# One decoder step on one core: the second value projection is moved from ahead of the attention to among its first scores

## The chip, the cores and the metric

The kernel runs on one core of one Trainium2 chip. The metric is device time in microseconds (us) of one launch. Besides the times there is one profiled execution of the kernel before, and all instants below ("at 628.7") are microseconds from the start of the span of that execution.

## The reference, cut to what matters

A prompt of 512 positions and 8 single-token samples (520 columns together, `T`) go through two layers of width 1024. The part that matters here is the start of the second layer: keys and values are made once from a normed hidden state, queries from another one, and 16 query heads share 4 key/value heads within a window of 128.

```python
hk = rmsnorm(h, kv_norm_g)
k = rope_partial((hk @ w_k).reshape(B, T, N_KV_HEADS, HEAD_DIM), pos)
v = (hk @ w_v).reshape(B, T, N_KV_HEADS, HEAD_DIM)
hn = rmsnorm(h, norm_mix_g[i])
q = rope_partial((hn @ w_q[j]).reshape(B, T, N_HEADS, HEAD_DIM), pos)
o = swa_prompt(q, k, v, sinks[j])        # window 128, softmax with a sink per head
h = h + o @ w_o[j]
```

Before it stand a gated short convolution, a feed-forward block and a gated per-layer embedding; after it another feed-forward block, another gate and a last norm. All of it is in the changed kernel as it was.

## The kernel before, in words

**Products.** Every matrix product is made of three single-pass products of split operands (high with high, high with low, low with high). `dense` (L192) loads one 128-column tile of weights by a DMA from the SP queue into one of three `raw` buffers, and splits it in halves of four 128x128 blocks: ACT casts the high part (L180), DVE subtracts for the low part (L162). The split halves lie in a ring of four `pair` buffers, so that a tile's first half can be split when the tile two before it has been used up that far. TensorE (PE) then runs 8 k-steps of 6 matmuls (128x260): 48 matmuls a tile. `ps2` hands out the accumulation banks A, B, C in rotation; once `banks["tags"]` is "AB" (L969) it hands out A and B alone, and C holds attention scores (`s`).

**The stretch around the change.** In order: two key tiles (`k0`, `k1`, L735); two value tiles (`v0`, `v1`, L750) from the same input `kx`; four transpositions of the first value tile (`vsplit`, L758, tile `vps`); query tiles `q0` to `q3` (L963) from input `mx`; then the attention of the first half of the heads. A finished value tile is multiplied by the norm's factor `r` on DVE into `vt` (L753), and its last columns are written out by a DMA. Keys and queries are turned by `rope` (L711): a shuffle and a product on DVE, a product and a sum on POOL (for `q2` and `q3` on DVE instead), then a split of the result by two casts on ACT and two subtractions on DVE (`ksplit` L723 into `kk` and `kk1`, `qsplit` L780). The tiles `q2` and `q3` are first copied from their bank by ACT (`to_sbuf`, L204, tiles `q2s`, `q3s`).

**The attention** goes in units u = 0 to 15 (8 for each half of the heads): scores on PE (L805), mask and row maximum on DVE (L810), exponentials on ACT (L822), normalising on ACT (L831) and POOL (L833), transpositions on PE (`pt`, L843), their split on ACT and DVE (`PT`, L844 and L845), and the products with the values (`av`, L856). Query tiles `q4` to `q7` are filler there: `steps` (L928) is a generator that yields after each k-step, and `pump(n)` runs n steps of it. `AHEAD` says how many steps come before the first score, `FILL` how many at each of four places of each unit. At u = 6 what is left of them is run, and the second value tile is transposed. The second half of the heads (u = 8 on) needs `kk1` and the queries `q4` to `q7`. The output projections (`o`, L960) fill units 8 on.

**What sets the order.** The program is written in this order; a scheduler then sets the order in which the instructions stand on each engine, and each engine runs its own in that order.

Of the kernel before, what the change touches and what calls it, by code (L numbers as in the profile page):

```python
# [23 lines left out]
KD = D // 128  # L24
# [23 lines left out]

AHEAD = 7
FILL = ((1, 3, 1, 9), (1, 0, 0, 0), (0, 2, 2, 1), (0, 1, 0, 1),  # L50
# [9 lines left out]
def _program(nc, a, o):  # L60
# [3 lines left out]
    with tile.TileContext(nc) as tc, ExitStack() as ctx:  # L64
# [297 lines left out]
        for j in range(KD):  # L362
            pc = pc1 if j == 1 else dense(a["w_in"][3 * j], cx, f"pc{j}") if j else None
            px_ = dense(a["w_in"][3 * j + 1], cx, f"px{j}") if j else None
            if j == 0:
                r = nm.r
# [311 lines left out]
        px, pe, nq = ffn(0, fx, nf)  # L678
        kx, mx = dpairs(KD, 0, "kx"), dpairs(KD, 7, "mx")
        nk = Norm("k")  # L680
# [68 lines left out]
        preload(AF.Exp, kt32[0])  # L749
        for p in range(2):  # L750
            pv = dense(a["w_v"][p], kx, f"v{p}")
            t = cp.tile([128, T], F32, tag="r2", name="vt1") if p else temp("vt0")
            V.tensor_tensor(halves(t), pv, halves(r), ALU.mult)  # L753
            nc.sync.dma_start(o["vw"][:, p, :], t[:, S - WIN:])
            G.tensor_copy(vsm[:, p, :], t[:, S:])
            vt.append(t)

        def vsplit(p, tag):  # L758
# [169 lines left out]
        def steps(tiles):  # L928

            def load(i):
                w, _, name = tiles[i][:3]
                raw = wr.tile([128, 8, 128], F32, tag="raw", name=f"{name}r")
                nc.sync.dma_start(raw[:, :w.shape[1]], w)
                return raw[:, :w.shape[1]]

            def cast(raw, k, name):
                pr = wp.tile([128, 2, 4, 128], F32R, tag="pair", name=f"{name}p{k}")
                A.copy(pr[:, 0], raw[:, k:k + 4])  # L940
                V.tensor_tensor(pr[:, 1], raw[:, k:k + 4], pr[:, 0].bitcast(F32), ALU.subtract)
                return [(pr[:, 0, i, :], pr[:, 1, i, :]) for i in range(4)]

            n = len(tiles)
            raws = [load(0), load(1)]
            ws = [p for k in range(0, raws[0].shape[1], 4) for p in cast(raws[0], k, tiles[0][2])]
            yield
            for i, (_, xs, name, done) in enumerate(tiles):
                ps, cur, ws = ps2(name), ws, []
                if i + 2 < n:  # L950
                    raws.append(load(i + 2))
                for k in range(len(cur)):
                    dense_k(ps, cur, xs, k)
                    if i + 1 < n and k in (1, 3) and 4 * (k // 2) < raws[i + 1].shape[1]:
                        ws += cast(raws[i + 1], 4 * (k // 2), tiles[i + 1][2])
                    if k == len(cur) - 1:
                        done(ps[:, :, :TH])
                    yield
# [4 lines left out]
        for t_ in range(4):  # L963
            if t_ == 2:
                kk1 = ksplit(1, [[cp.tile([128, T], F32R, tag=g, name=f"kk1{g}") for g in gs]
                                 for gs in (("tabc", "tabs"), ("acc", "r"))], kt32[1])
            pq_ = dense(a["w_q"][t_], mx, f"q{t_}")
            qsplit(t_, qrope(t_, to_sbuf(pq_, f"q{t_}s") if t_ > 1 else pq_))
        banks["tags"] = "AB"  # L969
        o0 = otiles(0, "D3", "D10")  # L970

        pending = []
# [7 lines left out]
        def add_h(m):  # L980
            return lambda ps: later(1, V.tensor_tensor, halves(h[m]), halves(h[m]), ps, ALU.add)

        gen = steps([(a["w_q"][t_], mx, f"q{t_}", q_done(t_)) for t_ in range(4, 8)]
                    + [wo_tile(0, m, *o0, add_h(m)) for m in range(KD)])
        next(gen)
        left = 4 * KD

# [7 lines left out]
        def pump(n):  # L995
# [4 lines left out]
            left -= min(n, left)  # L1000

        att = [Attn(0, kk0, vv0, *o0), None]
        samples = [sample(0, "X6", "X7", *o0), None]
# [13 lines left out]

        pump(AHEAD)
        each("score", 0)
# [195 lines left out]
```

## Time and profile before

| | us |
|---|---|
| median of 3 runs (lowest to highest) | 1227.99 (1227.5 to 1228.44) |
| the profiled execution's own time | 1226.76 |
| its span, first to last instruction | 1225.0 |
| PE busy / idle in the span | 1201.0 / 24.0 |
| DVE, ACT, POOL busy | 876.2, 630.9, 112.9 |
| mean granted clock of TensorE | 0.994 |

A granted clock of 1.00 is TensorE's 2.4 GHz, 0.50 its 1.2 GHz. The page's shares are means over the whole kernel; the change touches some 120 us of it, from the key projections at 605 to the last score that needs a query tile at 712.

### The profile page before, as it was taken

The numbers are of one execution on the slowest core, as the hardware profiler recorded it, in microseconds if no ns is written. First come the engines' busy times: TensorE is split into PE (matmuls) and PEld (weight loads), VectorE is DVE, ScalarE is ACT, GpSimd is POOL, SyncE is SP. The second block draws the span as 40 slices with busy tenths as digits, with TensorE's granted clock in tenths as the row PEclk, the third lists the DMA queues.
The fourth block names the chain that finished last, engine by engine and source line by source line (L and its number), as shares of the span: only waits on it lengthen the run. The fifth ranks groups of instructions, "written<-read, shape, count | busy, mean of one in ns | idle before, by whom it ended". The sixth has DMA issues, their size and how long they took to land.

```text
span 1225.0 us, 23933 instructions
## 1 busy us (share of the span) xinstructions
PE 1201.0 (98%) x9805; PEld 1183.9 (97%) x9805; DVE 876.2 (72%) x1509; ACT 630.9 (52%) x1073; POOL 112.9 (9%) x155
## 2 busy tenths in 40 slices
PE   9999999999999999999998989999999999999996
PEld 8999999999999999999998979999999999999996
DVE  6845557877777873678788777787776779428955
ACT  6323244555555842465655787654555567226631
POOL 2000000101010000111033321000101010001000
PEclk9999999999999999999999999999999999999998
DMA  6223323856655342744631131346666643248302
GB/s 217 87 87 96 97 87 106 214 147 155 157 156 139 92 127 91 204 99 116 185 114 53 39 92 53 113 119 184 154 159 154 161 99 115 93 132 210 116 1 70
DMA packets 56862, 149.69 MB, mean 122 GB/s; under 512 B 5680, under 2 KB 18992, under 8 KB 56752
## 3 DMA queue, kind: packets, MB, share of 16 engines
q1 hardware_dynamic: 46144, 117.66, 30.6%
q0 software_dynamic: 10464, 30.46, 13.6%
q8 instruction: 77, 1.26, 0.4%
q14 instruction: 33, 0.27, 0.1%
q10 hardware_dynamic: 144, 0.03, 0.0%
HBM read 113.10 MB, written 4.58 MB: 96 GB/s over the span
## 4 chain that ended last, share of the span: by engine, by line
PE 87%; DVE 7%; ACT 2%; DMA 1%; issue 1%; POOL 1%; SPq 0%; DVEq 0%; ACTq 0%; POOLq 0%
PE d L189 13%; PE pb L503 12%; PE pd L503 8%; PE pa L503 8%; PE o L189 4%; PE pg L189 4%; PE po L189 4%; PE g L189 4%; PE u L189 4%; PE pg L214 3%; PE pc L189 3%; PE pb L189 3%; PE px L189 3%; PE pbd L503 3%; PE pdd L503 2%; PE pad L503 1%
## 5 line engine op out<-in xcount | busy, mean ns | idle before, releaser
L503 PE MATMUL pb<-xs,wh 128*128 128x260 f32 x864 | 158.9, 283 | 0.0
L503 PEld LDWEIGHTS pb<-xs,wh 128*128 128x128 f32 x864 | 133.4, 188 | 0.0
L162 DVE TENSOR_TENSOR wl<-s,wh 128x1024 fp32r<-128x1024 f32 x72 | 88.0, 1223 | 37.4 <-PE pb L503 27.7
L453 ACT CAST wh<-s 128x1024 fp32r<-128x1024 f32 x72 | 75.7, 1051 | 73.1 <-PE pd L503 53.8
L503 PE MATMUL pd<-xs,wh 128*128 128x260 f32 x576 | 106.9, 285 | 0.2 <-DVE u L512 0.2
L503 PE MATMUL pa<-xs,wh 128*128 128x260 f32 x576 | 105.3, 283 | 0.0
L503 PEld LDWEIGHTS pd<-xs,wh 128*128 128x128 f32 x576 | 88.7, 188 | 1.8 <-DVE u L512 0.4
L503 PEld LDWEIGHTS pa<-xs,wh 128*128 128x128 f32 x576 | 88.8, 188 | 0.0
L503 PE MATMUL pb<-xs,wl 128*128 128x260 f32 x288 | 81.5, 283 | 0.0
L503 PE MATMUL pd<-xs,wl 128*128 128x260 f32 x288 | 81.4, 283 | 0.0
L503 PEld LDWEIGHTS pd<-xs,wl 128*128 128x128 f32 x288 | 54.2, 188 | 0.0
L503 PEld LDWEIGHTS pb<-xs,wl 128*128 128x128 f32 x288 | 54.2, 188 | 0.0
L503 PE MATMUL pa<-xs,wlE 128*128 128x260 f32 x144 | 40.7, 283 | 0.0
L503 PE MATMUL pa<-xs,wl 128*128 128x260 f32 x144 | 40.7, 283 | 0.0
L503 PE MATMUL pb<-xs,wlE 128*128 128x260 f32 x144 | 40.6, 282 | 0.0
L512 DVE TENSOR_TENSOR u<-pd,u 128x520 f32<-128x520 f32 x36 | 25.0, 695 | 21.7 <-PE pd L503 21.7
L160 POOL DMA_DIRECT2D wlE<-w1r x18 | 15.4, 857 | 229.4 <-ACT wlE L159 229.4
L453 ACT CAST wh<-w3r 128x1024 fp32r<-128x1024 f32 x18 | 18.9, 1052 | 26.9 <-PE pb L503 26.9
L822 ACT ACTIVATE P<-P,nmx 128x256 f32<-128x256 f32 (+1 forms) x64 | 30.2, 475 | 2.3 <-DVE nmx L814 2.2
L453 ACT CAST wh<-w1r 128x1024 fp32r<-128x1024 f32 x18 | 18.9, 1052 | 22.2 <-PE pb L503 22.2
L214 PE MATMUL pg<-px1D,wg 128*128 128x260 f32 x216 | 28.5, 284 | 0.0
L503 PEld LDWEIGHTS pa<-xs,wlE 128*128 128x128 f32 x144 | 27.2, 189 | 0.0
(1066 smaller groups left out, 3372.4 us busy)
## 6 DMA issues: line engine op xcount, KB each, us to landing
w1r<-in_w_gu SPq DMA_DIRECT2D x18, 512.0 KB, 3.5
w0r<-in_w_gu SPq DMA_DIRECT2D x18, 512.0 KB, 3.6
w2r<-in_w_gu SPq DMA_DIRECT2D x18, 512.0 KB, 3.5
wlE<-w1r POOLq DMA_DIRECT2D x18, 512.0 KB, 5.6
w3r<-in_w_gu SPq DMA_DIRECT2D x18, 512.0 KB, 3.6
wlE<-w3r POOLq DMA_DIRECT2D x18, 512.0 KB, 4.5
h<-in_xT SPq DMA_DIRECT2D x8, 260.0 KB, 5.6
xs<-xn POOLq DMA_DIRECT2D x4, 520.0 KB, 6.6
```

What stands on the lines that cost most here:

```text
L160: G.dma_start(out=dst, in_=src, accum_op=ALU.add)
L162: V.tensor_tensor(dst, src, hi.bitcast(F32), ALU.subtract)
L189: TE.matmul(ps[:, c, :TH], l, r[:, c * TH:(c + 1) * TH], start=(k == 0 and i == 0), stop=(k == len(ws) - 1 and i == 2))
L214: TE.matmul(ps, l, r[:, cols], start=(k == 0 and i == 0), stop=(k == n - 1 and i == 2))
L453: A.copy(hi, src)
L503: TE.matmul(ps[:, e, :TH], w[l][:, e, k, :], x[r][:, k, :], start=(start and k == 0 and q == 0), stop=(k == 3 and q == 2), skip_group_chec ...
L512: V.tensor_tensor(dst, ps, src, ALU.add)
L822: A.activation(P[:, j, :w], P[:, j, :w], AF.Exp, bias=nmx[:, j:j + 1], accum_out=sm[:, j:j + 1])
```

## The change

- `v1` is no longer computed behind `v0`. It is the first tile of the generator `steps`, ahead of `q4`. What is done with a finished value tile is now a function, `vout`, called by hand for `v0` and by the generator for `v1`.
- `AHEAD` is 8, the 8 k-steps of `v1`; `FILL` has 5 steps where it had 3 in its first row. The generator has 40 steps before the output projections (`left = 5 * KD`) where it had 32.
- The input `kx` now lies in E2 to E5, D3 and D10, where it lay in E2 to E5, E0, E1 and D3. E0 and E1 are the buffers of the attention's `P`. The attention's output buffers (D3 and D10, `otiles`) are taken only behind the 8 steps.
- A part of `kk1` lies in a new buffer "r3" and not in that of `r`, which `v1` still reads.

```diff
--- before.py
+++ after.py
@@ -46,8 +46,8 @@
 
 
 
-AHEAD = 7
-FILL = ((1, 3, 1, 9), (1, 0, 0, 0), (0, 2, 2, 1), (0, 1, 0, 1),
+AHEAD = 8
+FILL = ((1, 5, 1, 9), (1, 0, 0, 0), (0, 2, 2, 1), (0, 1, 0, 1),
         (1, 2, 4, 1), (0, 2, 0, 6), (2, 0, 0, 1), (9, 0, 0, 6),
         (2, 5, 4, 0), (6, 0, 1, 3), (0, 0, 1, 3), (0, 1, 1, 2),
         (0, 1, 0, 1), (0, 2, 2, 3), (1, 0, 0, 2), (1, 0, 0, 1),
@@ -676,7 +676,8 @@
             po = dense(a["w_out"][m], yx, f"po{m}")
             resid(m, po, nf, (N_FFN0,), (fx,))
         px, pe, nq = ffn(0, fx, nf)
-        kx, mx = dpairs(KD, 0, "kx"), dpairs(KD, 7, "mx")
+        kx = dpairs(4, 0, "kx") + dpairs(2, 6, "kx") + dpairs(2, 13, "kx")
+        mx = dpairs(KD, 7, "mx")
         nk = Norm("k")
         pg = {}
         for i in range(KD + 1):
@@ -747,13 +748,15 @@
             prep(mx[k], N_MIX1, k)
         vt = []
         preload(AF.Exp, kt32[0])
-        for p in range(2):
-            pv = dense(a["w_v"][p], kx, f"v{p}")
+
+        def vout(p, pv):
             t = cp.tile([128, T], F32, tag="r2", name="vt1") if p else temp("vt0")
             V.tensor_tensor(halves(t), pv, halves(r), ALU.mult)
             nc.sync.dma_start(o["vw"][:, p, :], t[:, S - WIN:])
             G.tensor_copy(vsm[:, p, :], t[:, S:])
             vt.append(t)
+
+        vout(0, dense(a["w_v"][0], kx, "v0"))
 
         def vsplit(p, tag):
 
@@ -941,17 +944,16 @@
                 V.tensor_tensor(pr[:, 1], raw[:, k:k + 4], pr[:, 0].bitcast(F32), ALU.subtract)
                 return [(pr[:, 0, i, :], pr[:, 1, i, :]) for i in range(4)]
 
-            n = len(tiles)
             raws = [load(0), load(1)]
             ws = [p for k in range(0, raws[0].shape[1], 4) for p in cast(raws[0], k, tiles[0][2])]
             yield
             for i, (_, xs, name, done) in enumerate(tiles):
                 ps, cur, ws = ps2(name), ws, []
-                if i + 2 < n:
+                if i + 2 < len(tiles):
                     raws.append(load(i + 2))
                 for k in range(len(cur)):
                     dense_k(ps, cur, xs, k)
-                    if i + 1 < n and k in (1, 3) and 4 * (k // 2) < raws[i + 1].shape[1]:
+                    if i + 1 < len(tiles) and k in (1, 3) and 4 * (k // 2) < raws[i + 1].shape[1]:
                         ws += cast(raws[i + 1], 4 * (k // 2), tiles[i + 1][2])
                     if k == len(cur) - 1:
                         done(ps[:, :, :TH])
@@ -963,12 +965,10 @@
         for t_ in range(4):
             if t_ == 2:
                 kk1 = ksplit(1, [[cp.tile([128, T], F32R, tag=g, name=f"kk1{g}") for g in gs]
-                                 for gs in (("tabc", "tabs"), ("acc", "r"))], kt32[1])
+                                 for gs in (("tabc", "tabs"), ("acc", "r3"))], kt32[1])
             pq_ = dense(a["w_q"][t_], mx, f"q{t_}")
             qsplit(t_, qrope(t_, to_sbuf(pq_, f"q{t_}s") if t_ > 1 else pq_))
         banks["tags"] = "AB"
-        o0 = otiles(0, "D3", "D10")
-
         pending = []
 
         def later(n, fn, *args):
@@ -980,10 +980,11 @@
         def add_h(m):
             return lambda ps: later(1, V.tensor_tensor, halves(h[m]), halves(h[m]), ps, ALU.add)
 
-        gen = steps([(a["w_q"][t_], mx, f"q{t_}", q_done(t_)) for t_ in range(4, 8)]
-                    + [wo_tile(0, m, *o0, add_h(m)) for m in range(KD)])
+        tiles = [(a["w_v"][1], kx, "v1", lambda ps: vout(1, ps))]
+        tiles += [(a["w_q"][t_], mx, f"q{t_}", q_done(t_)) for t_ in range(4, 8)]
+        gen = steps(tiles)
         next(gen)
-        left = 4 * KD
+        left = 5 * KD
 
         def run_pending(every=False):
             for job in pending:
@@ -999,6 +1000,9 @@
                 next(gen, None)
             left -= min(n, left)
 
+        pump(AHEAD)
+        o0 = otiles(0, "D3", "D10")
+        tiles += [wo_tile(0, m, *o0, add_h(m)) for m in range(KD)]
         att = [Attn(0, kk0, vv0, *o0), None]
         samples = [sample(0, "X6", "X7", *o0), None]
         event = 0
@@ -1015,7 +1019,6 @@
             if 0 <= u < 16:
                 getattr(att[u // 8], what)(u % 8, *args)
 
-        pump(AHEAD)
         each("score", 0)
         tick(-1, 0)
         each("exps", 0)
```

The scheduler's orders before and after differ from here to u = 8. On DVE, behind the ropes of the two key tiles (`v0p`, `q0p`: halves of split weights; `kk`, `kk1`: split keys; `vt`: a value tile), this stood before:

```order
L162 TENSOR_TENSOR v1p_7279<-v1r_7274,v1p_7279 128x512
L730 TENSOR_TENSOR kk_7343<-k0b,kk_7343 64x520 x2
L753 TENSOR_TENSOR vt_7269<-v_7212,rk 128x520
L730 TENSOR_TENSOR kk_7343<-k0b,kk_7343 64x520 x2
L162 TENSOR_TENSOR q0p_7355<-q0r_7353,q0p_7355 128x512
L162 TENSOR_TENSOR q0p_7358<-q0r_7353,q0p_7358 128x512
L730 TENSOR_TENSOR kk1tabs<-k_7186,kk1tabc 64x520
L162 TENSOR_TENSOR q1p_7424<-q1r_7422,q1p_7424 128x512
L730 TENSOR_TENSOR kk1tabs<-k_7186,kk1tabc 64x520
L753 TENSOR_TENSOR vt_7330<-v_7273,rk 128x520
L162 TENSOR_TENSOR q1p_7427<-q1r_7422,q1p_7427 128x512
L767 TENSOR_TENSOR vv_7334<-vps_7336,vv_7334 128x4x2x64
```

and this stands there now:

```order
L162 TENSOR_TENSOR q0p_7296<-q0r_7291,q0p_7296 128x512
L731 TENSOR_TENSOR kk_7281<-k0b,kk_7281 64x520 x2
L754 TENSOR_TENSOR vt_7268<-v_7211,rk 128x520
L731 TENSOR_TENSOR kk_7281<-k0b,kk_7281 64x520 x2
L162 TENSOR_TENSOR q1p_7362<-q1r_7360,q1p_7362 128x512
L770 TENSOR_TENSOR vv_7272<-vps_7274,vv_7272 128x4x2x64
L162 TENSOR_TENSOR q1p_7365<-q1r_7360,q1p_7365 128x512
L731 TENSOR_TENSOR kk1tabs<-k_7185,kk1tabc 64x520 x2
L731 TENSOR_TENSOR kk1r_7431<-k_7185,kk1acc 64x520 x2
L162 TENSOR_TENSOR q2p_7443<-q2r_7441,q2p_7443 128x512
L714 STREAM_SHUFFLE q0a<-q_7290 128x520
```

The half of `v1`'s weights has been replaced by that of `q0`, both stand-alone halves of `q0` and the second `vt` are gone from here, and the first `vt` has kept its place behind two splits of `kk`.

On PE, at the start of `q0`, this stood before:

```order
L189 MATMUL v_7273<-kxE_6314,v1p_7279 128x260 x6
L189 MATMUL v_7273<-kxD_6315,v1p_7279 128x260 x12
L764 MATMUL vps_7336<-ident,vt_7269 128x128 x4
L189 MATMUL q_7352<-mxD_6316,q0p_7355 128x260 x12
L189 MATMUL q_7352<-mxD_6317,q0p_7355 128x260 x12
```

and now:

```order
L189 MATMUL v_7211<-kxE_6312,v0p_7214 128x260 x6
L189 MATMUL v_7211<-kxD_6313,v0p_7217 128x260 x12
L189 MATMUL v_7211<-kxD_6314,v0p_7217 128x260 x12
L189 MATMUL q_7290<-mxD_6315,q0p_7293 128x260 x8
L767 MATMUL vps_7274<-ident,vt_7268 128x128 x4
L189 MATMUL q_7290<-mxD_6315,q0p_7293 128x260 x4
L189 MATMUL q_7290<-mxD_6316,q0p_7293 128x260 x12
```

The transpositions of `vt` stood behind all 48 matmuls of `v1`; now they stand behind 8 matmuls of `q0`.

On PE, from the last query tile of the first half to the next ones (`s` are scores, from one `q` each), this stood before:

```order
L189 MATMUL q_7573<-mxD_6318,q3p_7579 128x260 x12
L189 MATMUL q_7573<-mxD_6319,q3p_7579 128x260 x12
L805 MATMUL s_7707<-kk_7343,q_7416 128x128 x2
L805 MATMUL s_7707<-kk_7343,q_7485 128x128 x2
L189 MATMUL q_7656<-mxD_6316,q4p_7650 128x260 x12
L189 MATMUL q_7656<-mxD_6317,q4p_7650 128x260 x12
L189 MATMUL q_7656<-mxD_6318,q4p_7653 128x260 x12
L189 MATMUL q_7656<-mxD_6319,q4p_7653 128x260 x6
L805 MATMUL s_7707<-kk_7343,q_7568 128x128 x2
L805 MATMUL s_7707<-kk_7343,q_7639 128x128 x2
L189 MATMUL q_7656<-mxD_6319,q4p_7653 128x260 x6
L189 MATMUL q_7765<-mxD_6316,q5p_7671 128x260 x5
```

and now:

```order
L189 MATMUL q_7511<-mxD_6318,q3p_7517 128x260 x12
L808 MATMUL s_7655<-kk_7281,q_7354 128x128 x2
L808 MATMUL s_7655<-kk_7281,q_7423 128x128 x2
L189 MATMUL v_7592<-kxE_6309,v1p_7586 128x260 x6
L189 MATMUL v_7592<-kxE_6310,v1p_7586 128x260 x6
L189 MATMUL v_7592<-kxE_6311,v1p_7586 128x260 x6
L189 MATMUL v_7592<-kxE_6312,v1p_7586 128x260 x6
L189 MATMUL v_7592<-kxD_6313,v1p_7589 128x260 x12
L189 MATMUL v_7592<-kxD_6314,v1p_7589 128x260 x12
L808 MATMUL s_7655<-kk_7281,q_7506 128x128 x2
L808 MATMUL s_7655<-kk_7281,q_7577 128x128 x2
L189 MATMUL q_7675<-mxD_6315,q4p_7607 128x260 x12
```

and on DVE, from the rope of `q3` to the first mask, before:

```order
L714 TENSOR_TENSOR q3a<-q3a,rope 128x520
L941 TENSOR_TENSOR q5p_7686<-q5r,q5p_7686 128x512
L717 TENSOR_TENSOR q3b<-q3b,q3a 128x520
L786 TENSOR_TENSOR q_7639<-q3b,q_7639 64x520 x2
L941 TENSOR_TENSOR q6p_7780<-q6r,q6p_7780 128x512
L810 ISA P_7716,mxs_7717<-s_7707,mask 128x128
```

and now:

```order
L944 TENSOR_TENSOR q4p_7622<-q4r,q4p_7622 128x512
L718 TENSOR_TENSOR q3b<-q3b,q3a 128x520
L789 TENSOR_TENSOR q_7577<-q3b,q_7577 64x520 x2
L944 TENSOR_TENSOR q5p_7715<-q5r,q5p_7715 128x512
L754 TENSOR_TENSOR vt_7649<-v_7592,rk 128x520
L944 TENSOR_TENSOR q5p_7730<-q5r,q5p_7730 128x512
L813 ISA P_7664,mxs_7665<-s_7655,mask 128x128
```

`v1` has taken the place of `q4` behind the first scores, and its `vt` stands ahead of the first mask.

On PE, around the end of `q7`, this stood before:

```order
L189 MATMUL q_8119<-mxD_6319,q7p_8041 128x260 x12
L843 MATMUL pt_8272<-ident,P_8150 128x128 x4
L856 MATMUL av_8279<-PT_8180,vv_7334 128x512
L856 MATMUL av_8279<-PT_8181,vv_7334 128x512
L856 MATMUL av_8279<-PT_8180,vv_7334 128x512 x2
L856 MATMUL av_8279<-PT_8181,vv_7334 128x512
L856 MATMUL av_8279<-PT_8180,vv_7334 128x512
L805 MATMUL s_8304<-kk_7343,q_7416 128x256 x2
L805 MATMUL s_8304<-kk_7343,q_7485 128x256 x2
L805 MATMUL s_8304<-kk_7343,q_7568 128x256 x2
L843 MATMUL pt_8297<-ident,P_8150 128x128 x4
L805 MATMUL s_8304<-kk_7343,q_7639 128x256 x2
```

and now:

```order
L189 MATMUL q_8210<-mxD_6317,q7p_8079 128x260 x12
L846 MATMUL pt_8254<-ident,P_8101 128x128 x4
L189 MATMUL q_8210<-mxD_6318,q7p_8079 128x260 x12
L859 MATMUL av_8278<-PT_8131,vv_7272 128x512
L859 MATMUL av_8278<-PT_8132,vv_7272 128x512
L859 MATMUL av_8278<-PT_8131,vv_7272 128x512 x2
L859 MATMUL av_8278<-PT_8132,vv_7272 128x512
L859 MATMUL av_8278<-PT_8131,vv_7272 128x512
L846 MATMUL pt_8296<-ident,P_8101 128x128 x4
L808 MATMUL s_8303<-kk_7281,q_7354 128x256 x2
L808 MATMUL s_8303<-kk_7281,q_7423 128x256 x2
L808 MATMUL s_8303<-kk_7281,q_7506 128x256 x2
```

One group of four transpositions (`pt`) stood behind the last of `q7` and stands ahead of its last 12 matmuls now.

## Rows read from the trace of the kernel before

**Rows 1.** Busy time by engine, from the page (share of the span, instructions).
```profile
PE 1201.0 (98%) x9805; PEld 1183.9 (97%) x9805; DVE 876.2 (72%) x1509; ACT 630.9 (52%) x1073; POOL 112.9 (9%) x155
```

**Rows 2.** Busy time in four stretches: stretch, its length, engines, PEclk, DMA share, GB/s.
```profile
604.00:655.89 51.89, 50.73 (x423) 50.18 (x421) 44.47 (x78) 27.24 (x47) 15.60 (x16) 1.00 0.45 132
655.89:670.15 14.26, 12.14 (x96) 11.49 (x97) 11.99 (x38) 7.85 (x24) 5.66 (x9) 1.00 0.14 50
670.15:703.11 32.96, 32.85 (x240) 30.63 (x239) 25.31 (x93) 24.98 (x74) 11.83 (x19) 0.95 0.08 26
703.11:720.89 17.78, 13.76 (x82) 10.64 (x82) 15.55 (x55) 14.75 (x45) 6.85 (x13) 1.00 0.52 147
```

**Rows 3.** The three longest waits of PE, 620 to 722: total us, times, longest.
```profile
PE pt L843 <- ACT P L831: 2.5, 2, 2.0
PE pt L843 <- DVE PT L845: 2.2, 4, 1.0
PE q L189 <- ACT q3s L204: 1.0, 1, 1.0
```

**Rows 4.** Timeline of PE, 625 to 643: start, length, what, [idle before, releaser].
```profile
625.10 4.50 PE L189 MATMUL v<-kxE,v1p 128*128 128x260 f32 x36
...
630.87 0.60 PE L764 MATMUL vps<-ident,vt 128*128 128x128 f32 x4
631.23 5.97 PE L189 MATMUL q<-mxD,q0p 128*128 128x260 f32 x48
637.04 5.92 PE L189 MATMUL q<-mxD,q1p 128*128 128x260 f32 x48
```

**Rows 5.** Timeline of DVE, 625 to 638.
```profile
625.40 2.27 DVE L730 TENSOR_TENSOR kk<-k0b,kk 64x520 fp32r<-64x520 f32 x2 [0.31 <-ACT kk L728]
627.71 0.70 DVE L753 TENSOR_TENSOR vt<-v,rk 128x520 f32<-128x520 f32 x1
...
630.17 1.29 DVE L162 TENSOR_TENSOR q0p<-q0r,q0p 128x512 fp32r<-128x512 f32 x2
...
637.39 0.75 DVE L713 STREAM_SHUFFLE q0a<-q 128x520 f32<-128x520 f32 x1
```

**Rows 6.** Instructions of L764: the semaphore that its weight loads pass (lengths, instants).
```profile
L764 PEldq EVENT_SEMAPHORE  x1: 51/51/51, 628.7 to 628.7; - x1
```

**Rows 7.** Timeline of PE, 654 to 660.
```profile
654.35 0.56 PE L805 MATMUL s<-kk,q 128*128 128x128 f32 x4
655.89 4.33 PE L189 MATMUL q<-mxD,q4p 128*128 128x260 f32 x34 [0.98 <-ACT q3s L204]
```

**Rows 8.** Timeline of ACT, 653 to 656.
```profile
653.94 1.28 ACT L784 CAST q<-q2b 64x520 fp32r<-64x520 f32 x2 [1.62 <-DVE q2b L717]
655.24 0.59 ACT L204 COPY q3s<-q 128x520 f32<-128x520 f32 x1
```

**Rows 9.** First unit: the split of q3 and the first mask (DVE), the first transposition (PE).
```profile
659.90 1.42 DVE L786 TENSOR_TENSOR q<-q3b,q 64x520 fp32r<-64x520 f32 x2 [0.69 <-ACT q L784]
...
661.95 0.28 DVE L810 CUSTOM_DVE_ANT_0 P<-s,mask 128x128 f32<-128x128 f32 x1
...
669.22 0.33 PE L843 MATMUL pt<-ident,P 128*128 128x128 f32 x1 [1.98 <-ACT P L831]
```

**Rows 10.** From the end of q7: its rope (DVE, POOL), its split (DVE), transpositions of u = 6 (PE).
```profile
703.22 0.75 DVE L713 STREAM_SHUFFLE q7a<-q 128x520 f32<-128x520 f32 x1
...
705.44 1.29 POOL L717 TENSOR_TENSOR q7b<-q7b,q7a 128x520 f32<-128x520 f32 x1
...
710.66 0.69 DVE L786 TENSOR_TENSOR q<-q7b,q 64x520 fp32r<-64x520 f32 x1
...
713.12 0.66 PE L843 MATMUL pt<-ident,P 128*128 128x128 f32 x4 [1.02 <-DVE PT L845]
```

**Rows 11.** PE and the granted clock where it fell: timeline row, then a stretch of 5 us.
```profile
693.88 1.85 PE L920 MATMUL pse<-sst,vc 128*128 128x8 f32 x16
...
695.00:700.00 5.00, 5.00 (x30) 4.81 (x30) 3.38 (x8) 3.31 (x11) 0.53 (x1) 0.66 0.02 3
```

## The prediction

> **What bounds the kernel now.** I read the page's busy times first: PE is busy for 1201.0 of 1225.0 us [rows 1], so the time is that of PE's work plus some 24 us of gaps, and an edit that moves work pays only as far as it closes gaps. Then the stretches around the change, to see where these gaps lie [rows 2]. From the key projections to the start of `q4` (604 to 655.89) PE lacks 51.89 - 50.73 = 1.2 us; from there to the first transposed unit it lacks 2.1; in the 33 us behind that, filled by query tiles, 0.1; and from the end of `q7` to the last score that is late (703.11 to 720.89) 4.0. Together 7.4 us. Then the waits of PE, to see who ends them [rows 3]: the longest is 2.0 us for the first normalised `P`; 1.0 for the copy of `q3` out of its bank; 2.2 us in four waits for splits of transposed units on DVE, which lie behind the end of `q7`. Last the timelines of PE, DVE and ACT at the two seams that the change opens. The stretch that loses `v1` hardly waits on PE (1.2 us), while DVE is busy for 44.5 of its 51.9 us [rows 2]: what matters there is whether DVE keeps up when PE has less to do.
>
> **The change part by part.** All sums are against the profiled execution: span 1225.0 us, own time 1226.76, which is 1.8 more than the span. Its time is 1.2 below the median of the three runs, 1227.99; I add the difference to the median.
>
> (1) `v1` leaves its old place. PE ran it from 625.10 to 630.87 [rows 4]: -5.8 us there, +5.8 us at its new place, with the same 48 matmuls. If nothing waited, only the gaps would count.
>
> (2) A new wait at the transpositions of `v0`. They read `vt`. DVE makes it at 627.71 to 628.41 [rows 5], and PE's semaphore for it came at 628.7 [rows 6], hidden by `v1`, which ran until 630.87. Nothing ahead of `vt` on DVE gets shorter by the change: the order has the same row count there, half a split of `q0` standing where half a split of `v1` stood, and both splits of `kk` still ahead of `vt`. So `vt` comes at 628.7 again. PE now has only 8 matmuls of `q0` as cover: 8 x 0.12 us (5.81 us for 48, [rows 4]) = 1.0 from 625.10, so it stands at 626.1 and waits 2.6 us. Queued behind are the other 40 matmuls of `q0` and all query tiles. The bounds are 2.3 and 2.9.
>
> (3) The wait for the copy of `q3` grows. From `vt` on, DVE loses two halves of `q0` (1.29 us) and the second `vt` (0.70, as the first) ahead of the rope of `q0` [rows 5]: it starts 2.0 us earlier, at 635.4. From there to `q3` the chain goes through DVE, POOL and ACT in the old order, one link waiting for the other, so it stays 2.0 us earlier. The copy of `q3` was done by ACT at 655.24 to 655.83, straight behind the casts of `q2`, which had been waiting for DVE [rows 8]; now it ends at 653.8. PE comes sooner: 628.7, plus the transpositions (0.4), 40 matmuls (4.8), three tiles (17.3, from 637.04 to 654.35, [rows 4, 7]) and two pairs of scores (0.5) is 651.7. `v1` gets the bank that `q4` had there, that of `q3`: by the rotation the banks of both have moved by one. So PE waits from 651.7 to 653.9, 2.2 us, where it waited 0.98 [rows 7]: +1.2. The bounds are 0.5 (POOL and ACT gain a little) and 1.9.
>
> By (1) to (3) `v1` starts at 653.9, where `q4` started at 655.89. PE is 2.0 us ahead with 5.8 us more to do: 3.8 us behind. These must come out of the 6.2 us of gaps that lie further on.
>
> (4) The first unit. The split of `q3`, which ended at 661.3 [rows 9], ends at 659.3; half a split of `q5`, `vt` of `v1` and the other half (0.7 each, as [rows 5, 9]) then stand ahead of the first mask, which so starts at 661.4 and not 661.95. From it to the first transposition took 7.3 us [rows 9]. Four DVE instructions of about 0.7 us on `q4` and `q6` that stood in between are behind it now, so at most 7.3 and at least 4.5 us are left: 665.9 to 668.7. PE, with `v1` to 659.65, then the rest of the first scores (0.5), the second unit's (1.0) and 36 matmuls of `q4` (4.3), is there at 665.4, so it lacks 0.5 to 3.3. I take 1.0, nearer the lower end since all four pieces are out of the way; part of it falls ahead of the second unit's scores, which need the first masks done. 1.0 in place of 2.1: -1.1, bounds -1.6 and +1.2. `vsm` on POOL and the DMA of `vt` on SP move here too; behind the DMA on SP are only the loads of the output weights, which are first used behind the end of `q7`. They cost nothing.
>
> (5) The filled part to the end of `q7`. PE was busy for 32.85 of 32.96 us, DVE for 25.3 [rows 2]. It gets the matmuls that `v1` has displaced, and stays bound by PE. No gap is there to be closed, so the rest of the debt passes through. One group of `pt` (0.4) is pulled ahead of the end of `q7`. New gaps of 0 to 1 us may open; I take 0.
>
> (6) Behind `q7`. There the scores of unit 8 need the split of `q7`: its rope starts on DVE at 703.22, POOL ends it at 706.7, the split stands on DVE at 710.66, and the next transpositions at 713.12, 10.0 us from the end of `q7` [rows 10]. That chain is what PE waits for there. In the new order DVE has less in front of the split (two halves of output weights have gone ahead), but POOL has a normalising pair before the sum of the rope, and ACT splits `q7` ahead of the values' copy. I take the same 10 us. The 4.0 us of gaps [rows 2] then remain, and the group of `pt` that went ahead is lost: +0.3. Bounds -1.5 (most of the 2.2 us of waits for DVE in [rows 3] go) and +0.8.
>
> Sum: 2.6 + 1.2 - 1.1 + 0.3 = **+3.0 us**. Span 1228.0, own time 1229.8, against the median 1231.0.
>
> **The rivals.** *The clock.* Between 695 and 700 the granted clock was 0.66 on average, TensorE being at its 1.2 GHz level for some 3.4 us (0.34 x 5 / 0.5), behind 16 matmuls of 8 columns that took 1.85 us [rows 11]; the loss is 0.34 x 5 = 1.7 us. The sample's products have other neighbours now. If the fall is gone, +3.0 - 1.7 = +1.3: 1229.3. It can go the other way: the waits in (2) and (3) are longer than the 1.98 us at 667 [rows 9], behind which the clock stayed at 1.00 [rows 2]. If it falls behind the second, `v1` runs at half the rate and the time is +3.0 + 1.7 = +4.7, 1232.7; a fall behind the first would mostly be hidden in the wait of (3). As the trace shows no fall behind a single gap of 2 us, this case gets little. [...]
>
> *Faster.* The debt of 3.8 us is paid out of the gaps if the first unit no longer waits (-2.1) and unit 8 is no longer late (-4.0), and with fuller work the clock doesn't fall (-1.7): -4.0, 1224.0. It decides from where more than 3.8 us are recovered. For it speaks that DVE has 2 us less ahead of the attention. Against it speak the 0.1 us of gaps in the filled part: what `v1` adds there is only added, and `q7` ends later, on which unit 8 hangs. The Trainium skill ("Perfetto Trace Analysis", section "Optimization Strategy") says that interleaving stretches with different bounds may improve a kernel; by that rule this case would be the likeliest, and the rows of the filled part don't bear it out.
>
> That the change doesn't do what it says is excluded by the order: `v1` does stand among the scores.
>
> **How the numbers follow.** The forecast, +3.0 with its own range of +1.6 to +4.4 (1229.6 to 1232.4), gets 0.52. No fall of the clock, +1.3: 0.20. One more fall, +4.7: 0.13. The faster case: 0.15. A measurement can tell 0.2% from no change, 2.46 us here, so 1225.5 and 1230.5 are the limits. The forecast gives slower 0.34 and same 0.18; the second same 0.18 and slower 0.02; the third slower 0.13; the fourth faster 0.12 and same 0.03. Faster 0.12, same 0.39, slower 0.49. The range of 8 in 10 goes from 1225.6, which leaves out most of the faster case, to 1233.2.
>
> **What would show it.** (2): a wait of PE of 2.3 to 2.9 us at `vps` for DVE. (3): a wait of `v1` for the copy of `q3` of 1.5 to 2.9 us. (4): the gap ahead of the first `pt` under 1.2 us. (5): a stretch without gaps, ending some 3 us later by `q7`. (6): scores of unit 8 and `pt` about 10 us behind `q7`. It is wrong if `vt` comes before 627, if the rope of `q0` gains more than 2 us, or if the gaps behind `q7` shrink below 2.5 us.

## The result: slower, by more than was forecast

The changed kernel took 1237.74 us (median of three runs, 1237.64 to 1237.87) where the kernel before took 1228.22 (four runs, 1227.5 to 1229.35): the ratio is 1.0071, 95% interval 1.0052 to 1.0091. A fourth run of the changed kernel, at a granted clock of 0.844, took 1296.41 us and is not counted. Forecast was 1231.0, in a range up to 1233.2. The sign was right and the time lies outside the range. Three further series of the same two kernels, told below, gave 1.0042 (1.0027 to 1.0057), 1.0042 (1.0029 to 1.0054) and 1.0049 (1.0033 to 1.0064). By these three ratios the change costs some 5 to 6 us. The first series lies at the upper end of the spread that the later ones show (1231.16 to 1237.88); why all three of its runs do is not shown.

The profiled execution of after has a span of 1235.9 us, own time 1237.64 (before: 1225.0 and 1226.76). From its page, the busy times by engine:

```profile
PE 1208.6 (98%) x9805; PEld 1190.5 (96%) x9805; DVE 877.3 (71%) x1509; ACT 631.0 (51%) x1073; POOL 112.4 (9%) x155
```

Against [rows 1] the number of instructions is the same, and PE is busy for 7.6 us longer with the same matmuls: some of them ran slower. The same four stretches as in [rows 2], with their ends where the same things happen now (`v1` starts, start of the first transposed unit, end of `q7`, first scores of unit 10; [rows 2] cut at the end of the first transposed unit, 0.9 us further on):

```profile
604.00:653.83 49.83, 45.18 (x374) 44.40 (x372) 42.46 (x75) 25.80 (x45) 14.96 (x15) 1.00 0.42 125
653.83:667.34 13.51, 13.29 (x96) 13.07 (x97) 9.58 (x35) 5.94 (x17) 2.38 (x6) 0.87 0.22 73
667.34:710.20 42.86, 41.37 (x291) 38.23 (x290) 31.86 (x104) 29.78 (x90) 15.52 (x24) 0.92 0.07 22
710.20:730.08 19.88, 15.36 (x79) 12.19 (x78) 13.99 (x51) 13.03 (x39) 6.53 (x12) 0.83 0.47 141
```

The first has 4.6 us without PE work where it had 1.2; the second has lost its gap but runs at a granted clock of 0.87; the third and the fourth have 0.92 and 0.83 where [rows 2] have 0.95 and 1.00. The longest waits of PE in after, 620 to 731 (total us, times, longest):

```profile
PE s L808 <- DVE mxs L813: 2.9, 2, 2.6
PE v L189 <- ACT q3s L204: 2.3, 1, 2.3
PE vps L767 <- DVE vt L754: 2.2, 1, 2.2
PE pt L846 <- DVE PT L848: 1.9, 3, 0.9
PE pt L846 <- ACT P L834: 0.7, 1, 0.7
PE pse L923 <- DVE ssov L920: 0.7, 1, 0.7
```

The second and third are the two that the prediction had announced; the first, 2.63 us ahead of the first scores of unit 8, it had not. The granted clock of after, in stretches cut around its falls (a fall is a time in which it stands at 0.50):

```profile
651.00:655.00 4.00, 1.72 (x15) 1.58 (x14) 3.84 (x8) 2.46 (x4) 0.59 (x1) 1.00 0.43 131
655.00:659.00 4.00, 4.00 (x23) 4.00 (x22) 3.28 (x6) 1.76 (x3) 1.30 (x4) 0.57 0.23 74
695.00:700.00 5.00, 4.69 (x22) 4.41 (x23) 2.05 (x8) 2.12 (x8) 0.00 (x0) 0.62 0.14 52
700.00:704.00 4.00, 4.00 (x25) 4.00 (x24) 2.55 (x7) 2.44 (x8) 0.95 (x1) 0.62 0.00 0
720.00:724.00 4.00, 3.30 (x12) 2.32 (x11) 3.36 (x14) 3.29 (x12) 0.55 (x2) 0.51 0.02 8
724.00:728.00 4.00, 4.00 (x21) 3.61 (x21) 1.63 (x9) 2.91 (x12) 0.63 (x2) 0.63 0.00 0
1174.00:1178.00 4.00, 3.73 (x19) 3.73 (x20) 3.01 (x8) 2.90 (x8) 0.00 (x0) 0.57 0.00 0
```

A stretch of 4 us at 0.57 has lost 0.43 x 4 = 1.7 us, TensorE being at its 1.2 GHz level for 3.4 of it. By this count after loses 1.7 behind the wait of `v1`, 3.4 around 700, 3.4 behind unit 8's wait and 1.7 at 1174, where before lost 1.7 in all (besides the end of the kernel, where both fall alike).

Two theories were set against each other: that the *clock* is what was missed (each new wait costs its length and a fall behind it), and that the *chain* of ropes, masks and copies is later, the low clock being hidden in its waits.

### The profile page after: what moved, and what is told of

Same layout as the page of the kernel before. It is cut to its first block, busy times and chain, and to the rows that moved or that the text cites. A ratio compares the mean times of both kernels' runs of the same rounds, so it can differ in the third digit from the quotient of the medians.

```text
span 1235.9 us, 23930 instructions
## 1 busy us (share of the span) xinstructions
PE 1208.6 (98%) x9805; PEld 1190.5 (96%) x9805; DVE 877.3 (71%) x1509; ACT 631.0 (51%) x1073; POOL 112.4 (9%) x155
## 4 chain that ended last, share of the span: by engine, by line
PE 88%; DVE 6%; ACT 2%; issue 1%; DMA 1%; POOL 1%; SPq 0%; DVEq 0%; POOLq 0%; ACTq 0%
PE d L189 13%; PE pb L503 12%; PE pd L503 8%; PE pa L503 8%; PE o L189 4%; PE pg L189 4%; PE po L189 4%; PE g L189 4%; PE u L189 4%; PE pg L214 3%; PE pc L189 3%; PE pb L189 3%; PE px L189 3%; PE pbd L503 3%; PE pdd L503 2%; PE av L859 1%
## 5 line engine op out<-in xcount | busy, mean ns | idle before, releaser
L214 PEld LDWEIGHTS pg<-px1D,wg 128*128 128x128 f32 x216 | 27.9, 195 | 0.0
```

What stands on the lines that cost most here:

```text
L214: TE.matmul(ps, l, r[:, cols], start=(k == 0 and i == 0), stop=(k == n - 1 and i == 2))
```

## The experiments

**The same program again.** Three times, on three chips, beside the kernel before.

> The changed kernel once more, unaltered, on this chip beside the kernel before, for the spread from run to run. Theory clock: runs of one and the same program differ by how many falls of the granted clock they meet (1.7 us of loss each), so the times spread over 3 us or more, go up as the granted clock goes down, and span times granted clock stays within 1 us of 1219.9 (of before: about 1217.5). Theory chain: the clock tells nothing, span times granted clock spreads as far as the span itself.

> The changed kernel a third time, unaltered. Theory clock: the same waits as in the two profiles before (2.2 at vps, 2.6 at unit 8's scores, within 0.2 us), but falls of the granted clock behind another choice of them; times from 1231 to 1238 that go up as the clock goes down, and span times clock at 1220 to 1221.5. Theory chain: the time of a run doesn't follow its clock.

> The changed kernel a fourth time, unaltered, as the measure for the run beside it: 1233 to 1235 median, granted clock 0.987 to 0.993 over the runs.

| series | changed, median (runs) | before | ratio, 95% | clock, changed | clock, before |
|---|---|---|---|---|---|
| a0 | 1233.06 (1231.78 to 1233.49) | 1229.43 | 1.0042 (1.0027 to 1.0057) | 0.992 | 0.989 to 0.995 |
| a1 | 1234.2 (1231.16 to 1237.88) | 1229.08 | 1.0042 (1.0029 to 1.0054) | 0.987 to 0.993 | 0.990 to 0.995 |
| a2 | 1235.71 (1232.95 to 1236.09) | 1228.81 | 1.0049 (1.0033 to 1.0064) | 0.989 to 0.992 | 0.989 to 0.994 |

The ratios are those on record; the medians of the table alone would give 1.0029, 1.0042 and 1.0056, or 3.6, 5.1 and 6.9 us. Runs of one program differ by several us, and the time follows the clock: over the 19 runs of the changed kernel in this table a thousandth of mean clock goes with 0.9 us (correlation -0.86), over the 50 of before with 0.8 us (-0.89). The three profiles have the waits of after (2.2 at `vps`, 2.6 ahead of unit 8), but other falls. In a1, the same places as above:

```profile
654.00:658.00 4.00, 4.00 (x21) 4.00 (x21) 3.27 (x8) 1.22 (x3) 0.55 (x3) 0.57 0.15 30
695.00:700.00 5.00, 4.56 (x36) 4.43 (x37) 3.28 (x13) 3.52 (x12) 0.00 (x0) 1.00 0.18 52
1173.00:1177.00 4.00, 4.00 (x36) 4.00 (x35) 2.89 (x8) 1.54 (x4) 0.00 (x0) 1.00 0.00 0
```

and in a0, where the fall came behind the wait at `vps` instead:

```profile
628.00:633.00 5.00, 4.93 (x29) 4.93 (x30) 4.90 (x9) 3.60 (x7) 1.11 (x3) 0.66 0.91 229
654.00:658.00 4.00, 4.00 (x35) 4.00 (x34) 3.31 (x6) 1.21 (x3) 0.86 (x4) 1.00 0.13 13
```

In a0 the wait of `v1` was 0.8 us, not 2.3: PE, slowed ahead of it, came later, so 1.5 of the 1.7 us were hidden. After and a1 are one program with nearly the same waits. From the start of `v0` to the end of `q7` they take 91.0 and 87.8 us: the difference is the long fall around 700 (a loss of 3.4). Behind unit 10 after, with the fall at 1174, takes 505.8 and a1 504.6. Behind `q7` they take 19.9 and 19.8, with losses of 3.4 and 1.7: there the second half of the fall is hidden in the waits. No profile of the changed kernel is without a fall at that place, so what the first half costs is an estimate, some 0.4 us: from the `pt` at 718.91 to the one at 723.96 a1 takes 5.05, and before takes 4.69 for the same groups without a fall (713.12 to 717.81). So a1 against before is, but for these 0.4, the change with as many falls on the path as before, and it is 6.7 us longer in span (1231.7).

**The layout alone.**

```diff
-        kx, mx = dpairs(KD, 0, "kx"), dpairs(KD, 7, "mx")
+        kx = dpairs(4, 0, "kx") + dpairs(2, 6, "kx") + dpairs(2, 13, "kx")
...
-                                 for gs in (("tabc", "tabs"), ("acc", "r"))], kt32[1])
+                                 for gs in (("tabc", "tabs"), ("acc", "r3"))], kt32[1])
```

> The kernel before with nothing but the new places of kx and of kk1's second part, without any move of work. If the new places cost nothing (transfers and copies that wait for a place), the time is that of before, 1228.2 within 0.4 us, and the clock 0.99. If they cost, part of the 9.5 us shows here: 1229.5 or more.

1229.12 beside 1230.04, ratio 0.9996 (0.9981 to 1.0010): the new places cost nothing that can be told (1.2 us at most by the interval). Its profile, of the old order of work, taught something else. The wait of 1.98 us ahead of the first `pt`, behind which the clock stayed at 1.00 in [rows 2], is there too, and this time it fell (timeline of PE, then a stretch):

```profile
668.69 0.33 PE L844 MATMUL pt<-ident,P 128*128 128x128 f32 x1 [1.98 <-ACT P L832]
```
```profile
668.00:674.00 6.00, 5.31 (x29) 5.03 (x30) 3.98 (x16) 4.52 (x17) 2.42 (x4) 0.72 0.00 0
```

**The wait at `vps` alone.** The kernel before, with `v1` ahead of `v0` and nothing else moved.

```diff
-        for p in range(2):
+        for p in (1, 0):
             pv = dense(a["w_v"][p], kx, f"v{p}")
```

> The kernel before with the two value projections in the other order, v1 first, so that vps waits for DVE's vt as in the changed kernel and nothing else moves. Theory of a wait bound by PE: a wait of 2.2 us at vps, the end of q7 2.2 us later than before, 1.5 to 2.5 us over the kernel before. Theory that the ropes set the pace: the wait of 0.98 at q4 for ACT's copy of q3 and that of 2.0 at the first pt shrink, and the time is that of before within 0.7 us.

1230.85 beside 1228.81, ratio 1.0014 (1.0005 to 1.0024), so +1.7 us (0.6 to 2.9). Its profile has the wait, and a fall behind it:

```profile
634.12 0.66 PE L764 MATMUL vps<-ident,vt 128*128 128x128 f32 x4 [2.17 <-DVE vt L753]
```
```profile
634.00:639.00 5.00, 4.88 (x28) 4.88 (x29) 3.07 (x6) 1.21 (x2) 0.58 (x1) 0.66 0.58 182
```

`q3`'s first scores come at 658.30, 3.95 later than in [rows 7]: 2.2 for the wait and 1.7 for the fall, here at a place where PE sets the pace. The waits for `q3` (0.79) and for the first `pt` (1.97) are nearly those of before (0.98 and 1.98), so the ropes did not pay it back.

**The early waits in the changed kernel.** First `v1` in the other pair of banks, so that it doesn't wait for ACT's copy of `q3`; then the turning of `v0` behind `q0`; then both.

```diff
         banks["tags"] = "AB"
+        banks["i"] += 1
```
```diff
-        vv0 = vsplit(0, "D9")
...
+            if t_ == 0:
+                vv0 = vsplit(0, "D9")
             qsplit(t_, qrope(t_, to_sbuf(pq_, f"q{t_}s") if t_ > 1 else pq_))
```

> The changed kernel with v1 put into the other pair of banks, the one that q1 has left, so that v1 no longer waits for ACT's copy of q3 (2.28 us in the changed kernel, with the granted clock down at 655.4 to 658.7 behind it, a loss of 1.7 us). Theory clock: a gap costs its own length and then the lower clock, so both go, and the end of q7 comes 2.3 + 1.7 = 4 us earlier, less what the chain over the first unit's mask and probabilities takes back (up to 2 us): 1233.5 to 1236 against 1237.7. Theory chain: the wait at v1 only stands in for the chain q3, rope, scores, mask, probabilities, whose end stays where it is; then the wait turns up again ahead of the first pt, the clock falls there instead, and the time is 1237 to 1238.

> The changed kernel with the turning of v0 (the four transposes into vps with both copies) written behind q0's products instead of ahead of them, so that PE doesn't wait for DVE's vt (2.22 us). Theory bound by PE: q0 to q3 run 2.2 us earlier with no new wait, 1235.5. Theory bound by the ropes: the wait at v1 for ACT's copy of q3 grows from 2.3 to 3.5 to 4.5 us, since the ropes on DVE and POOL don't come earlier, and the time is 1237 to 1238. Under the clock theory the lower clock behind v1's wait stays in both.

> Both edits, v1 in the other banks and the turning of v0 behind q0. Theory clock: no gap of 2 us is left ahead of the first unit, so the fall at 655 goes, and 2.2 + 4 us less up to 3 us that the first unit takes back are saved: 1231.5 to 1234.5. Theory chain: the end of the first unit's chain moves little, one long wait of 4 us or more stands ahead of the first pt, 1236 to 1238.

1232.66, 1235.08 and 1233.02, beside 1230.04: ratios 1.0029 (1.0016 to 1.0042), 1.0052 (1.0034 to 1.0071), 1.0024 (1.0012 to 1.0037). These were judged against 1237.7, the changed kernel's first time, before it was known how far that spreads; beside 1.0042 to 1.0049 the first and third lie 1.5 to 3 us lower, but on another chip and with intervals that overlap, so the times show no gain for any of the three. What the traces say is plainer. The timelines of PE, from e1, e2 and e3 in this order:

```profile
658.22 0.44 PE L808 MATMUL s<-kk,q 128*128 128x128 f32 x2 [1.06 <-DVE q L789]
661.11 1.11 PE L808 MATMUL s<-kk,q 128*128 128x128 f32 x8 [1.08 <-DVE mxs L813]
```
```profile
652.68 5.38 PE L189 MATMUL v<-kxE,v1p 128*128 128x260 f32 x24 [4.20 <-ACT q3s L204]
```
```profile
657.52 0.44 PE L807 MATMUL s<-kk,q 128*128 128x128 f32 x2 [2.92 <-DVE q L788]
```

In e1 the wait of 2.28 comes back as two of 1.1 for the split of `q3` and for the mask. In e2 PE comes to `v1` 2.5 us earlier, counted from the start of `v0`, and waits 4.2 us for the copy of `q3`, as the theory of the ropes had it. In e3 it waits 2.9 for the split of `q3`. The first `pt` comes 46.2 us behind the start of `v0` in e1 and 46.1 in e3, where the changed kernel has 46.6 with its fall hidden (a0). The chain over the ropes sets the first unit, and `v1` at its new place doesn't close that gap; PE only stands in another spot of it.

**Behind `q7`.** In after, ACT, DVE and PE there:

```profile
715.98 1.27 ACT L787 CAST q<-q7b 64x520 fp32r<-64x520 f32 x2 [2.51 <-POOL q7b L718]
717.28 0.59 ACT L769 CAST vv<-vps 128x512 fp32r<-128x512 f32 x1
717.90 0.69 DVE L770 TENSOR_TENSOR vv<-vps,vv 128x512 fp32r<-128x512 f32 x1 [2.39 <-ACT vv L769]
718.50 0.41 DVE L813 CUSTOM_DVE_ANT_0 P<-s,mask 128x256 f32<-128x256 f32 x1
718.98 0.33 PE L808 MATMUL s<-kk1tabc,q 128*128 128x128 f32 x1 [2.63 <-DVE mxs L813]
```

ACT's copy of the turned values (`vv`) stands behind the casts of `q7`, which wait 2.5 us for POOL's rope; DVE's half of `vv` waits for it, unit 7's fourth mask stands behind that, and unit 8's scores need the bank that this mask reads. Here `q7` ends, and unit 10's scores begin (timeline of PE in after):

```profile
708.54 1.68 PE L189 MATMUL q<-mxD,q7p 128*128 128x260 f32 x12
...
730.08 0.28 PE L808 MATMUL s<-kk1tabc,q 128*128 128x256 f32 x1
```

The edit turns `v1` one unit earlier:

```diff
+            if u == 5:
+                vv1 = vsplit(1, "D5")
             if u == 6:
                 pump(left)
                 run_pending(True)
-                att[1] = Attn(1, kk1, vsplit(1, "D5"), None, None)
+                att[1] = Attn(1, kk1, vv1, None, None)
```

> The changed kernel with the turning of v1 (transposes into the second vps and both copies to vv) written one unit earlier, ahead of the sixth unit instead of behind q7, so that ACT's copy to vv no longer stands behind the casts of q7 that wait for POOL. Theory late copy: the fourth mask of unit 7 comes at 715.4 instead of 718.5, the wait of 2.63 us of unit 8's scores falls under 1.2 us, the way from the end of q7 to pt of (unit 6, second half) is 10 us again instead of 11.3, and with the clock's fall behind it (3.4 us of loss) gone 1233 to 1236. Theory rope: unit 8's scores need q7's rope, which POOL ends at 716 anyway, so the wait stays over 2 us with another name, and the time is 1236.5 to 1238.

1231.91 beside 1229.43, ratio 1.0030 (1.0015 to 1.0046), 1.2 us under a0 on the same chip, which the intervals don't separate. The trace does: the copy comes at 707.92, the fourth mask at 714.05, and unit 8 waits 0.6 (timelines of ACT, DVE and PE):

```profile
707.92 0.56 ACT L769 CAST vv<-vps 128x512 fp32r<-128x512 f32 x1
```
```profile
714.05 0.41 DVE L813 CUSTOM_DVE_ANT_0 P<-s,mask 128x256 f32<-128x256 f32 x1
```
```profile
707.20 1.69 PE L189 MATMUL q<-mxD,q7p 128*128 128x260 f32 x12
...
714.53 0.33 PE L808 MATMUL s<-kk1tabc,q 128*128 128x128 f32 x1
...
716.01 0.33 PE L808 MATMUL s<-kk1tabc,q 128*128 128x128 f32 x1 [0.59 <-DVE q L789]
717.72 0.66 PE L846 MATMUL pt<-ident,P 128*128 128x128 f32 x4 [0.20 <-DVE PT L848]
...
726.17 0.28 PE L808 MATMUL s<-kk1tabc,q 128*128 128x256 f32 x1
```

From the end of `q7` to unit 10's scores it is 17.3 us, where all four profiles of the changed kernel have 19.8 to 20.0; e7 and a1 (19.8) each have a fall of one length there. The theory of the late copy holds; that of the rope doesn't. The same edit in the kernel before:

> The kernel before with the turning of v1 one unit earlier, the edit that took the wait of 2.63 us out of the changed kernel. In the kernel before, ACT's copy to vv stands between the two casts of q7 at 707.7 and unit 7's fourth mask ends at 710.6, with no wait of unit 8's scores over 0.6 us. If the copy's place matters only where it stands behind both casts: within 0.3 us of before. If it holds the mask up here too: 0.5 to 1.5 us under before.

1227.12 beside 1229.08, ratio 0.9985 (0.9976 to 0.9994): this one beats the kernel before by 2.0 us at the median, and the changed one with it. The stretch behind `q7` took 17.0 us in its profile and 17.8 before, so about 0.8 of the 2.0 lies there; the rest may be the clock (0.992 to 0.995 over its ten runs), which wasn't tried.

The other edit at this place gave PE zeros to multiply ahead of unit 8's scores.

> The changed kernel with 40 matmuls of 128 columns on zeros put ahead of unit 8's first scores, where PE waits 2.63 us for unit 7's mask; nobody reads what they write. No wait is taken away, PE only has something to do in it. Theory clock: the fall at 720.5 to 726.9 (3.4 us of loss) goes, unit 8's scores start at 719 to 720 as before, 1233.5 to 1236.5. Theory chain: the lower clock there is hidden behind the chain over mask, ropes and probabilities, so nothing is won, 1237.5 to 1240.

1235.47, ratio 1.0061 (1.0046 to 1.0076), 2.4 us over a0 on the same chip. It settles nothing: the scheduler put a `pt` of unit 6 between the zeros and the scores, and its wait for DVE took the place of the wait for the mask (timeline of PE in e8).

```profile
713.40 2.24 PE L359 MATMUL busy<-zfill 128*128 128x128 bf16 x37
718.62 0.68 PE L855 MATMUL pt<-ident,P 128*128 128x128 f32 x4 [2.98 <-DVE PT L857]
```

**Waits filled with zeros.** In the two early waits (e4, the edit below), and then also with the turning of `v1` moved (e12, with 34 in place of 30).

```diff
+        busy(30)
         vv0 = vsplit(0, "D9")
...
+        busy(36)
         pump(AHEAD)
```

> The changed kernel with matmuls on zeros, whose results nobody reads, in its two early waits: 30 of 128 columns (about 1.8 us) ahead of vps, 36 (about 2.2 us) ahead of v1. The work that counts doesn't come earlier. Theory clock: with something to do there TensorE keeps 2.4 GHz through 625 to 660, where all four profiles of this stretch have a fall so far (three at 654, one at 629), so the end of q7 comes 1.7 us earlier than in those with the same falls behind it, and the time is 1 to 2 us under that of the changed kernel on this chip. Theory chain: the lower clock only shows where PE would wait anyway, so the time is that of the changed kernel or up to 1 us over it.

> The changed kernel with its two early waits filled by matmuls on zeros whose results nobody reads (34 ahead of vps, 36 ahead of v1) and with the turning of v1 one unit earlier, which took the wait of 2.63 us away. Theory clock: its runs have a mean clock of 0.992 to 0.995, like those of the kernel before at its best, with no fall between 620 and 665, and the times are 3 to 5 us under those of the changed kernel beside it (2.5 of them from the turning of v1). Theory that the falls come by chance and not from waits: mean clock 0.987 to 0.993 as in the changed kernel, and times 2 to 3 us under it.

e4: 1234.72, ratio 1.0035 (1.0022 to 1.0047); e12: 1233.25, ratio 1.0031 (1.0019 to 1.0044), 2.5 us under a2 beside it. In the profile of e4 there is no fall from 624 to 704:

```profile
624.00:629.00 5.00, 3.52 (x46) 3.29 (x45) 4.62 (x5) 4.15 (x8) 4.87 (x6) 1.00 0.27 86
628.00:633.00 5.00, 4.82 (x41) 4.82 (x42) 4.89 (x8) 3.75 (x7) 1.22 (x3) 1.00 0.92 237
654.00:658.00 4.00, 4.00 (x35) 4.00 (x34) 3.31 (x6) 1.21 (x3) 0.78 (x4) 1.00 0.16 26
695.00:704.00 9.00, 9.00 (x75) 8.87 (x75) 5.98 (x20) 5.03 (x13) 4.20 (x7) 1.00 0.11 32
```

and from `v0` to the end of `q7` it takes 86.7 us, 1.1 less than a1 with its one fall, though the work that counts came no earlier; a0, whose fall was hidden for the most part, takes 86.3 without any filling. In e12 none lies ahead of 680 either, but one comes behind the sample's 16 matmuls of 8 columns, where PE counts as busy all the time:

```profile
680.41 1.85 PE L908 MATMUL pse<-ssq,ks 128*128 128x8 f32 x16
```
```profile
682.00:686.00 4.00, 4.00 (x18) 3.58 (x18) 1.54 (x8) 0.72 (x2) 1.05 (x3) 0.57 0.00 0
```

Over the runs, the mean clock was 0.990 to 0.993 in e4 and 0.990 to 0.994 in e12, against 0.987 to 0.993 and 0.989 to 0.992 in the unfilled kernel beside each. The times show no gain from the filling: e4's 1234.72 stands beside a1's 1234.2 on the same chip, and the 2.5 us of e12 are what the turning of `v1` gives by the traces. So none of the four filled waits had a fall behind it, in one profile of each kernel (at `vps` 1.5 and 1.3 us stayed unfilled); that the filled kernel as a whole has fewer falls, these runs don't show, since there are other places where they come.

**Edits together.** Banks and turning of `v1`, and all three.

> Two of the edits in one, v1 in the other pair of banks (no wait for ACT's copy of q3) and the turning of v1 one unit earlier. If the two losses are independent: 1232.7 of the first edit alone, less 1 to 3 us: 1229.5 to 1232, span times granted clock 1217.5 to 1218.5, level with the kernel before. If the second edit wins nothing: 1232 to 1233.5.

> The changed kernel with all three edits: v1 in the other banks, the turning of v0 behind q0, the turning of v1 one unit earlier. Theory of three independent terms (2.2 at vps, 1.3 at v1, 2.5 behind q7, less what the first unit takes back): span times clock at 1215 to 1217.5, level with before or 1 us under it, time 1228 to 1230.5. If the rope chain sets the first unit: a wait of about 3 us ahead of the first scores stays, and the time is 1230 to 1232.

1231.46 beside 1229.43, ratio 1.0023 (1.0004 to 1.0043), and 1232.57 beside 1229.08, ratio 1.0028 (1.0012 to 1.0043). Both mend the stretch behind `q7` (17.6 us in each), and neither gets level with before: e11 keeps the wait of 2.9 for the split of `q3`, and its profile has falls at 658, 682, 716, 747 and 1170.

## Why the prediction fell short, step by step

I take a1 against the profile of before: one fall on the path in each, but for some 0.4 us in (6), and 6.7 us in span.

| step | forecast | measured |
|---|---|---|
| (2) wait at `vps` | +2.6 | +2.2 |
| (3) wait of `v1` for `q3s`, less 0.98 | +1.2 | +1.3 |
| (4) first unit | -1.1 | -2.0 at the first `pt`, +0.7 at the third: -1.3 |
| (5) filled part | 0 | +0.9 of waits, about +1.0 besides |
| (6) behind `q7` | +0.3 | +2.1 |
| behind unit 10 | 0 | +0.5 |
| sum | +3.0 | +6.7 |

*(1) to (4) held.* `v1` started at 653.83 where 653.9 was forecast, the first `pt` stood at 667.34 with a fall ahead of it, and at 665.59 in a0, where the fall was hidden (forecast 665.4). The wait at `vps` was a little under its bounds of 2.3 to 2.9; alone, in b3, it cost 2.2 on the path. The gain at the first `pt` was the whole 2.0, but 0.7 came back at the third transposed unit, whose `P` ACT ends late.

*(5) failed in size,* 0 against +1.9. The text allowed new gaps of 0 to 1 and took 0; there were 0.9 (0.63 ahead of the sample's products, 0.23 ahead of scores). Of the other 1.0, 0.4 is the group of `pt` that was expected ahead of the end of `q7`; the counts of the other matmuls up to there are those of before, and where the remaining 0.6 lies is not shown. No experiment took (5) apart.

*(6) is the step that failed most plainly,* +0.3 (bounds -1.5 and +0.8) against +2.1, with one group of `pt` less left in the stretch. The text saw that in the new order "ACT splits `q7` ahead of the values' copy" and then took "the same 10 us" from the end of `q7` to the next `pt` behind unit 8's scores; it was 11.7 in a1 (707.21 to 718.91), 11.2 in after and 8.8 in e7. It followed the chain of `q7` alone. Not followed was what the moved copy holds up: DVE's half of `vv`, the mask queued behind that on DVE, and the bank that this mask frees. e7 took this one thing away, and with it 2.5 us.

*The rival of one more fall failed in its chance.* "As the trace shows no fall behind a single gap of 2 us, this case gets little", 0.13. That was read from one execution. e5 has the same gap at the same place with a fall behind it, and the four profiles of the changed kernel have theirs behind the wait of `v1`, or behind that at `vps`, with no difference in the program. What the fall costs at either place was foreseen rightly: the whole 1.7 behind the wait of `v1` (after, a1), and little behind that at `vps`, where the wait of `v1` shrank from 2.3 to 0.8 (a0, a2). The Trainium skill ("TensorE: Matmul & The Clock Gate", section "HAM oscillation — how this bites in real kernels") tells of waits of PE behind which the clock is back at half rate; the waits of its example are longer than those of 1.3 to 2.3 us that had a fall behind them in after, e5 and b3, so the traces go further than the page. The length of a gap alone does not tell here whether a fall comes: 1.54 us at 1163 in before had none, 1.34 at 1173 in after had one.

```profile
1164.77 0.75 PE L214 MATMUL pj<-p,wj 128*128 128x260 f32 x4 [1.54 <-DVE tq L1096]
```
```profile
1164.00:1168.00 4.00, 3.23 (x26) 3.17 (x26) 3.36 (x9) 3.08 (x8) 0.00 (x0) 1.00 0.00 0
```
```profile
1174.27 1.23 PE L214 MATMUL pj<-p,wj 128*128 128x260 f32 x4 [1.34 <-DVE tq L1099]
```

*Between the profiles of before and after* lie 10.9 us of span. 6.7 are there in a1, more than twice the 3.0 of the sum; with 6.7 the forecast would have been 1234.7, already outside the range. The other 4.2 go with falls that a1 did not have (losses of 3.4 around 700 and of 1.7 at 1174, not all of them on the path). The +0.5 behind unit 10 was not looked into; there the four profiles of the changed kernel take 504.6 to 505.8, and before 504.1. Neither theory won alone. The faster case fell: the first unit was paid back, and the stretch behind `q7` got worse, not better. What stays open is which of the waits brings a fall in a given run; nothing in the program decides it in these traces.

## What to carry to other kernels

When an instruction is moved past others on its queue, follow not only its own chain but each instruction that now stands behind it on every engine, down to the buffer that the last one frees: here a copy of 0.6 us behind a cast that waits cost 2.5 us two engines further on. Work put into a gap closes it only if its own inputs and its bank are not at the end of the chain that makes the gap. And a clock that stayed up behind a gap in one profile is one draw: price each gap of PE by its length, and for the range by its length and the loss of one fall, 1.7 us in these traces.

## What was not expected of the hardware

Runs of one program on one chip spread over up to 7 us (1226.22 to 1232.88 for the kernel before in one series, 1231.16 to 1237.88 for a1) and follow the mean granted clock. Every fall ahead of the kernel's end, in all the profiles, had the same length, 3.4 us, or twice that, and a loss of 1.7 or 3.4 us. In the places read for this text they came in or right behind a wait of PE (1.3 to 4.2 us), or at the sample's 8-column matmuls, where PE's record shows no idle time in before and e12; in a1 the same matmuls had no fall.
